# An offset of its own, modulo 256 bytes, for each ring slot of split weight chunks

## The chip, the cores and the metric

The kernel runs on one core of a Trainium2 chip. The metric is the device time of one execution in microseconds (us); of several runs the median is given.

## What is computed

One decoder layer on 256 tokens of width 1024, all in float32. A SwiGLU feed-forward of width 2816, then a mixing layer with two branches side by side (a Mamba-2 state-space branch and a differential attention branch) that a sigmoid gate merges, then a second SwiGLU feed-forward. Around each stands an RMS norm before and one after. Cut to what matters:

```python
h = h + 0.5 * rmsnorm(swiglu(rmsnorm(h, ffn1_pre_g), w_gate, w_up, w_down), ffn1_post_g)
u = rmsnorm(h, mix_pre_g)
z, xbc, dt_raw, q, k, v, gate_logits = split(u @ w_in)
...
merged = gates[0] * y_ssd + gates[1] * y_att
h = h + rmsnorm(merged @ w_out, mix_post_g)
h = h + 0.5 * rmsnorm(swiglu(...), ffn2_post_g)
```

Almost all of the work is the product of the 256 tokens with some 32 million weights, each of which is read once from HBM.

## The kernel before, in words

**Precision by splitting.** A float32 product is made of three matmuls in the faster fp32r format. Each weight chunk and each activation is split into a high part, the value rounded to fp32r, and a low part, what the rounding left. Of the four products the three larger are added up: hi times hi, lo times hi and hi times lo.

**Weight chunks.** The weights come in chunks of 128 partitions by 2048 floats (8 KB per partition, 1 MB in all). For each chunk:
- `load` (L226) issues a DMA on SyncE's queue into a raw tile (L237).
- `hi` (L260) copies the raw tile to a tile `whi` on ScalarE, with rounding (L263).
- `lo` (L267) subtracts `whi` from the raw tile on VectorE and writes `wlo` (L270).
- `take` (L372) gives the pair to the matmuls, and has the next chunks prepared some way ahead.

There are 134 such pairs in the program; some (named `whiq` and `wloq`) come from sums of raw chunks, since part of the feed-forward uses a seven-product form (L309).

**The matmuls.** `mm_t` (L383, its matmuls on L390, L391 and L393) uses the chunk as the stationary operand and streams 256 token columns; 28 chunks in the mixing layer go that way. `mm_nat` (L395, its matmul on L404) and `mm_n` (L605, its matmul on L619) use the activations as the stationary operand and stream 512 columns of the chunk; the other 106 go that way.

**Where split chunks stand.** `ring` (L198) gives out the tiles. For each of the two kinds, `whi` and `wlo`, there are three slots of 8 KB per partition in the pool `sb`, which lives for the whole program, taken in turn. In the feed-forwards a fourth slot of each kind lies in the stage's own pool, and each fourth chunk of the kind goes there: 9 in each feed-forward. So of the 134 pairs 112 stand in the six slots of `sb`, 18 in the stages' slots, and 4, at the seams between stages, in half tiles of the stage (`blocks`, L245).

**Addresses.** Before the first `whi` slot and behind the last `wlo` slot `gap` (L195) puts a tile of 32 floats, 128 bytes, and has GpSimd set it to zero (L196). By the program's memory map the first gap begins at byte 84512 of each partition, which is 32 modulo 256. The starts of the tiles that matter here, modulo 256 (inside them matmuls, copies and subtractions begin at multiples of 256, but for the shifted reads of a convolution):

| tiles | start modulo 256 |
|---|---|
| three `whi` slots and three `wlo` slots in `sb` | 160 |
| raw tiles, the activations `u`, all tiles of the stage pools (the fourth slots, `gh`, `gl`, `v`, `sqy` and so on) | 160 |
| `k2` tiles (`sg`, `us`, `aT`, `wdt` and so on) | 224 |
| `h` and `ident` | 128 |
| `ones` | 192 |

**Order.** `own_order` (L427) has TensorE, ScalarE, VectorE and SyncE run in the order of the program text in the feed-forwards; GpSimd's queue is put in order by the framework's scheduler. In the mixing layer the scheduler orders more of the engines, up to L1383, where TensorE is taken into the text's order again. At the start GpSimd computes the inverse norms of the two token blocks (`rstd_of`, L502: L505 and L506), scales the second block (`unit`, L548: L551 `un_f`) and makes a diagonal (`diag`, L554); the gaps' zeros stand among these in its queue.

Of the kernel before, what the change touches and what calls it, by code (L numbers as in the profile page):

```python
# [14 lines left out]
F32 = mybir.dt.float32  # L15
F32R = mybir.dt.float32r
# [8 lines left out]
P = 128  # L25
T = 256
D = 1024
# [20 lines left out]
BG_US = 3.15  # L48
GATE_US = 1.35
SSD_US = 1.55  # L50
GROUPS = "hnsns"
BREAK, STOP = object(), object()

# [2 lines left out]
def tile_hybrid_layer(ctx: ExitStack, tc: tile.TileContext, x, ffn1_pre_g, ffn1_w_gate, ffn1_w_up,  # L56
# [4 lines left out]
    nc = tc.nc  # L61
    const = ctx.enter_context(tc.tile_pool(name="const", bufs=1))
    sb = ctx.enter_context(tc.tile_pool(name="sb", bufs=1))
# [69 lines left out]
    def ffn_chunks(wg, wu, wd):  # L133
# [3 lines left out]
        c0 = 512  # L137
        for kind in GROUPS:
            if kind == "h":
# [46 lines left out]
    raws, pairs, taken, rings = [], {}, [0], {}  # L186
# [5 lines left out]
    def mixing(c):  # L192
        return mix_first <= c < mix_last

    def gap(name):  # L195
        nc.gpsimd.memset(sb.tile([P, 32], F32, tag=name, name=name, bufs=1), 0.0)  # L196

    def ring(kind, n, more, name, c, dt=F32):  # L198

        first = kind not in rings  # L200
        i = rings.get(kind, 0) % (n + more)
        rings[kind] = rings.get(kind, 0) + 1
        if i < n or stage[1][1] != FFN_K4 or mixing(c):
            if first and kind == "whi":
                gap("gap0")
            t = sb.tile([P, 2 * D], dt, tag=kind, name=name, bufs=n)
            if first and kind == "wlo":
                gap("gap1")
            return t
        return stage[1][0].tile([P, 2 * D], dt, tag=kind, name=name, bufs=more)  # L210

    class Raw:
# [32 lines left out]
    def blocks(name, c, nj, nc_):  # L245

        if c in seams:
            n = nj // 2
            ts = [k4([P, n, nc_], f"{name}{q}", F32R) for q in range(2)]
            return lambda j, m: ts[j // n][:, j % n:j % n + m, :]  # L250
        t = ring(name[:3], SPLIT_BUFS, SPLIT_MORE, name, c, F32R).rearrange("p (j c) -> p j c", j=nj)
        return lambda j, m: t[:, j:j + m, :]
# [190 lines left out]
    h = const.tile([P, 2, D], F32, name="h")  # L443
# [35 lines left out]
    for name, v in (("mx", mix_pre_g), ("f2", ffn2_pre_g),  # L479
                    ("ng", ssd_norm_g), ("cb", ssd_conv_b), ("sg", da_subln_g)):  # L480
        n = v.shape[1] // P
# [236 lines left out]
    def ffn(post_v, tag, norm, ready, turned, then, at, ws=None, **kw):  # L718
# [21 lines left out]
        def later(n, f):  # L740
            due.append((slot[0] + n, f))
# [85 lines left out]
        for n, f in ((0, lambda: turned_back(sgs[0], 0, gh, gl)), (2, lambda: turned_back(sgs[1], 1, gh, gl)),  # L827
                     (8, then)):
            later(n, f)
        if "s" in GROUPS:  # L830
            for n in range(6):
                later(2 * n, lambda: next(making, None))
        else:
            norm.pu1 = norm.us = None
        for n, kind in enumerate(GROUPS):
            m = 2 if kind == "h" else 4
# [185 lines left out]
    dt = const.tile(shp, F32, name="dt")  # L1022
# [362 lines left out]
    def natural(name, n, hi, lo, evict, us, then=lambda: None):  # L1385


        accs = [pj(f"{name}{b}") for b in range(2)]
        for i in range(n):
            w = take()  # L1390
            for b in range(2):
                bs = slice(b * P, (b + 1) * P)
                mm_nat(accs[b], w, (lambda k: hi(k)[:, bs], lambda k: lo(k)[:, bs]), i * 4, i == 0, i == n - 1, "u")
                if i == n - 1:
                    evict(b, accs[b])
                back.run(us)
            if i == 0:
                then()
# [22 lines left out]
    for q in range(2):  # L1421
# [3 lines left out]

        natural(f"pws{q}", 4, lambda j: yh[j // 4][:, j % 4, :], lambda j: yl[j // 4][:, j % 4, :], gated, SSD_US)
    yh = yl = None
# [4 lines left out]
    def turn_merged(n):  # L1432

        for q, b, t, mh, ml in merges[:n]:
            pt = bg([P, 4, P], f"pmg{q}{b}")
            for m in range(4):
                nc.tensor.transpose(pt[:, m, :], t[:, m * P:(m + 1) * P], ident)
            bs = slice(b * P, (b + 1) * P)
            split(mh[:, :, bs], ml[:, :, bs], pt)
        del merges[:n]  # L1440
# [5 lines left out]
    for q in range(2):  # L1446
# [4 lines left out]
        def merge(b, acc):  # L1451
# [5 lines left out]
        natural(f"pwd{q}", 2, lambda j: oh[j // 4][:, j % 4, :], lambda j: ol[j // 4][:, j % 4, :], merge,  # L1457
                SSD_US if q == 0 else 0.0, (attended, lambda: turn_merged(2))[q])

# [51 lines left out]
```

## Time and profile before

| | |
|---|---|
| median of 3 runs | 765.84 us (765.19 to 766.61) |
| the profiled execution | 764.21 us |
| its span, from the first to the last instruction | 762.5 us |
| TensorE matmuls | 4113, busy 739.7 us (97%) |
| VectorE busy | 563.4 us (74%) |
| ScalarE busy | 431.3 us (57%) |
| GpSimd busy | 41.8 us (5%) |
| HBM traffic | 137 MB, 180 GB/s over the span |

The profile names the engines PE (TensorE, with PEld for its weight loads), DVE (VectorE), ACT (ScalarE), POOL (GpSimd) and SP (SyncE). L404 is line 404 of the kernel. A group of instructions has its line, engine and operation, output and inputs (`out<-in`; for a matmul the moving operand stands ahead of the stationary one), shape and count; then busy time in us, the mean length of one in ns, and the idle time of the engine ahead of them with what ended it. Matmuls overlap in the pipeline, so the mean length of one is longer than the time from one start to the next. In a piece of the chain or of the timeline the first number is the start in us, the second the length in us.

### The profile page before, as it was taken

Reading aid. Unit: us, or ns where it says so; the run is one execution under the profiler, and the core shown is the slowest. Engines: PE = TensorE matmul, PEld = TensorE weight load, DVE = VectorE, ACT = ScalarE, POOL = GpSimd, SP = SyncE. Lnnn points to the kernel's source line nnn. Section 1 sums busy time; section 2 is a strip of 40 time slices with the busy share of each in tenths; the row PEclk is TensorE's granted clock in tenths of the full one; section 3 lists DMA queues with packets and bytes.
Section 4 is the critical chain, followed back from the end, with each engine's and each line's share of the span. In section 5 each row is a group of like instructions: output and inputs, shape, how many; then the busy total and the mean of one; then the engine's idle time right before and its main releaser. Section 6 shows DMA issues by size and latency. Waiting matters only on the chain.

```text
span 762.5 us, 10271 instructions
## 1 busy us (share of the span) xinstructions
PE 739.7 (97%) x4113; PEld 628.7 (82%) x4113; DVE 563.4 (74%) x666; ACT 431.3 (57%) x583; POOL 41.8 (5%) x74
## 2 busy tenths in 40 slices
PE   8999899999989999999999999999999999999996
PEld 6878687788769999989999777888887888888885
DVE  6788897853657787777877878685777999988332
ACT  7543746743545455676967545685365657566321
POOL 6000000000141000000000000000013000000000
PEclk9999999999999999999999999999999999999999
DMA  8950755864345856565456454544565817549301
GB/s 315 318 200 0 272 169 169 336 210 141 111 125 181 263 179 182 176 190 160 139 174 191 161 198 135 191 164 133 201 221 166 282 50 248 193 167 358 110 1 55
DMA packets 77889, 137.92 MB, mean 181 GB/s; under 512 B 2749, under 2 KB 35601, under 8 KB 77841
## 3 DMA queue, kind: packets, MB, share of 16 engines
q1 hardware_dynamic: 75168, 129.51, 50.6%
q0 software_dynamic: 2368, 7.22, 3.2%
q8 instruction: 32, 0.52, 0.3%
q10 hardware_dynamic: 304, 0.53, 0.2%
q14 instruction: 17, 0.13, 0.0%
HBM read 136.17 MB, written 1.08 MB: 180 GB/s over the span
## 4 chain that ended last, share of the span: by engine, by line
PE 81%; DVE 7%; ACT 6%; issue 3%; POOL 1%; DMA 1%; SPq 0%; DVEq 0%; ACTq 0%; POOLq 0%
PE acc_f L619 15%; PE pu_f L404 6%; PE pg_f L404 5%; PE pws L404 5%; PE pgt L404 4%; PE pa_f L404 4%; ACT whi L263 3%; PE pn_f L404 3%; PE pwd L404 3%; DVE wlo L270 3%; PE pd_f L404 2%; PE pz L391 2%; PE pz L390 2%; PE pz L393 2%; PE pxs L391 2%
## 5 line engine op out<-in xcount | busy, mean ns | idle before, releaser
L270 DVE TENSOR_TENSOR wlo<-raw,whi 128x2048 fp32r<-128x2048 f32 (+2 forms) x116 | 243.5, 2109 | 94.3 <-ACT whi L263 92.7
L263 ACT CAST whi<-raw 128x2048 fp32r<-128x2048 f32 (+2 forms) x116 | 202.5, 1763 | 130.1 <-PE acc_f L619 38.0
L263 ACT CAST whiq<-raw 128x2048 fp32r<-128x2048 f32 x24 | 45.9, 1914 | 27.4 <-PE pu_f L404 11.3
L270 DVE TENSOR_TENSOR wloq<-raw,whiq 128x2048 fp32r<-128x2048 f32 x24 | 54.7, 2286 | 5.8 <-ACT whiq L263 5.8
L619 PE MATMUL acc_f<-whi,gh_f 128*128 128x512 f32 x160 | 51.6, 392 | 0.0
L619 PE MATMUL acc_f<-wlo,gh_f 128*128 128x512 f32 x160 | 51.3, 391 | 0.2 <-DVE wlo L270 0.2
L619 PE MATMUL acc_f<-whi,gl_f 128*128 128x512 f32 x160 | 51.4, 390 | 0.0
L404 PE MATMUL pgt<-whi,u_mx 128*128 128x512 f32 x128 | 35.1, 401 | 0.4 <-DVE gt L1415 0.4
L619 PEld LDWEIGHTS acc_f<-wlo,gh_f 128*128 128x128 f32 x160 | 29.9, 188 | 6.7 <-DVE wlo L270 0.6
L619 PEld LDWEIGHTS acc_f<-whi,gl_f 128*128 128x128 f32 x160 | 30.0, 188 | 6.2
L619 PEld LDWEIGHTS acc_f<-whi,gh_f 128*128 128x128 f32 x160 | 29.8, 188 | 6.2 <-ACT whi L263 0.2
L404 PE MATMUL pg_f<-whi,u_f 128*128 128x512 f32 x128 | 32.5, 397 | 1.2 <-DVE sg_f L777 1.2
L390 PE MATMUL pz<-u_mx,whi 128*128 128x256 f32 x128 | 32.0, 286 | 0.0
L391 PE MATMUL pz<-u_mx,whi 128*128 128x256 f32 x128 | 31.9, 286 | 0.0
L390 PE MATMUL pxs<-u_mx,whi 128*128 128x256 f32 x128 | 31.8, 286 | 0.0
L404 PE MATMUL pu_f<-whi,u_f 128*128 128x512 f32 x128 | 31.8, 391 | 0.0
L391 PE MATMUL pxs<-u_mx,whi 128*128 128x256 f32 x128 | 31.4, 283 | 0.0
L404 PEld LDWEIGHTS pg_f<-whi,u_f 128*128 128x128 f32 x128 | 23.4, 188 | 6.4 <-DVE sg_f L777 1.6
L404 PEld LDWEIGHTS pgt<-whi,u_mx 128*128 128x128 f32 x128 | 23.3, 188 | 6.4 <-issue 1.3
L404 PEld LDWEIGHTS pu_f<-whi,u_f 128*128 128x128 f32 x128 | 24.0, 188 | 5.0
L391 PEld LDWEIGHTS pz<-u_mx,whi 128*128 128x128 f32 x128 | 24.5, 192 | 0.5 <-issue 0.5
L390 PEld LDWEIGHTS pz<-u_mx,whi 128*128 128x128 f32 x128 | 24.5, 191 | 0.5 <-issue 0.5
(372 smaller groups left out, 1646.8 us busy)
## 6 DMA issues: line engine op xcount, KB each, us to landing
raw<-in_w_in_dram SPq DMA_DIRECT2D x40, 1024.0 KB, 5.3
raw<-in_ffn_w_down_dram SPq DMA_DIRECT2D x22, 1024.0 KB, 5.3
raw<-in_ffn_w_gate_dram SPq DMA_DIRECT2D x18, 1024.0 KB, 5.8
raw<-in_ffn_w_up_dram SPq DMA_DIRECT2D x18, 1024.0 KB, 5.2
raw<-in_ssd_w_branch_dram SPq DMA_DIRECT2D x8, 1024.0 KB, 5.0
raw<-in_ffn_w_up_dram SPq DMA_DIRECT2D x8, 512.0 KB, 5.8
acb<-acd POOLq DMA_DIRECT2D x8, 512.0 KB, 4.7
raw<-in_da_w_branch_dram SPq DMA_DIRECT2D x4, 1024.0 KB, 5.0
```

The lines of the kernel that those rows point to most:

```text
L263: i = nc.scalar.copy(got["hi"](j, step), src()[:, j:j + step, :])
L270: nc.vector.tensor_sub(got["lo"](j, step), src()[:, j:j + step, :], got["hi"](j, step).bitcast(F32))
L390: nc.tensor.matmul(acc[m], wh(j)[:, cs], ah(k0 + j), start=first and j == ks[0], stop=False)
L391: nc.tensor.matmul(acc[m], wh(j)[:, cs], al(k0 + j), start=False, stop=False)
L393: nc.tensor.matmul(acc[m], wl(j)[:, cs], ah(k0 + j), start=False, stop=last and j == ks[-1])
L404: nc.tensor.matmul(acc, a(k0 + j), b(j), start=first and i == 0, stop=last and i == 11, skip_group_check=go_on)
L619: nc.tensor.matmul(acc[b][q], x_[:, ts], w_(kt)[:, halves[q]], start=i == 0 and kt == 0 and x_ is ah and w_ is wh, stop=i == n - 1 and kt ...
```

## The change

The two gaps of 128 bytes become seven smaller ones, one ahead of each of the six slots and one behind the last. `STEPS` has their sizes in bytes, `GAP_END` the last. Each slot gets a tag of its own, with one buffer, and the slots are taken in turn by a counter of each kind. When a split chunk is first asked for, all gaps and all six slots are made at once (`home` tiles), so that they lie one behind the other, and the home tiles are then let go, so that the chunks take their places. The `whi` slots begin at 64, 96 and 128 modulo 256, the `wlo` slots at 192, 224 and 0. The gaps add up to 256 bytes as before.

```diff
+STEPS = {"whi": (32, 32, 32), "wlo": (64, 32, 32)}
+GAP_END = 32
...
-    def gap(name):
-        nc.gpsimd.memset(sb.tile([P, 32], F32, tag=name, name=name, bufs=1), 0.0)
+    homes, slots = {}, {k: 0 for k in STEPS}
+
+    def gap(name, size):
+        if size:
+            nc.gpsimd.memset(sb.tile([P, size // 4], F32, tag=name, name=name, bufs=1), 0.0)
 
     def ring(kind, n, more, name, c, dt=F32):
 
-        first = kind not in rings
         i = rings.get(kind, 0) % (n + more)
         rings[kind] = rings.get(kind, 0) + 1
         if i < n or stage[1][1] != FFN_K4 or mixing(c):
-            if first and kind == "whi":
-                gap("gap0")
-            t = sb.tile([P, 2 * D], dt, tag=kind, name=name, bufs=n)
-            if first and kind == "wlo":
-                gap("gap1")
-            return t
+            if kind not in STEPS:
+                return sb.tile([P, 2 * D], dt, tag=kind, name=name, bufs=n)
+            if not homes:
+                for k in STEPS:
+                    for slot in range(n):
+                        gap(f"gap_{k}{slot}", STEPS[k][slot])
+                        homes[k, slot] = sb.tile([P, 2 * D], F32R, tag=f"{k}{slot}", name=f"home_{k}{slot}", bufs=1)
+                gap("gap_end", GAP_END)
+                homes.update((h, None) for h in list(homes))
+            slot = slots[kind] % n
+            slots[kind] += 1
+            return sb.tile([P, 2 * D], dt, tag=f"{kind}{slot}", name=name, bufs=1)
         return stage[1][0].tile([P, 2 * D], dt, tag=kind, name=name, bufs=more)
```

## The prediction

> **What bounds the kernel now.** I read the page first: the busy shares, the granted clock and the chain that ended last.
>
> ```profile
> span 762.5 us, 10271 instructions
> PE 739.7 (97%) x4113; PEld 628.7 (82%) x4113; DVE 563.4 (74%) x666; ACT 431.3 (57%) x583; POOL 41.8 (5%) x74
> PEclk9999999999999999999999999999999999999999
> PE 81%; DVE 7%; ACT 6%; issue 3%; POOL 1%; DMA 1%; SPq 0%; DVEq 0%; ACTq 0%; POOLq 0%
> ```
>
> TensorE is busy 97% of the span, at full clock, and carries 81% of the chain. ScalarE and VectorE carry 13% of it. The question is therefore how fast TensorE runs in its long stretches, and whether an address could make that better or worse. Two pieces of the chain in order of time (start, length, what) say the first, and a count of the instructions of two lines (span, busy, number, for PE and PEld) says how many matmuls go at that pace.
>
> ```profile
> 147.61 49.47 PE acc_f L619 x218
> 302.33 0.96 PE pxs L393 x8
> ```
>
> ```profile
> 0.00:762.50 762.50, 377.46 (x1584) 292.70 (x1584) 1.00 0.54 181
> ```
>
> ```profile
> 0.00:762.50 762.50, 144.84 (x624) 116.41 (x624) 1.00 0.54 181
> ```
>
> The 218 matmuls of 512 columns take 49.47 / 218 = 0.227 us each, the ones of 256 columns 0.96 / 8 = 0.120 us. The slope between the two is 0.107 us for 256 columns, 2.4 columns per ns, and 0.013 us is a constant per matmul. So in a long stretch nothing is lost to a slow read: whatever is lost comes at breaks. Lines 404 and 619 together issue 1584 + 624 = 2208 matmuls of 512 columns; these read a split chunk as the moving operand. In the 256-column ones (L390 to L393) the chunk is the stationary operand.
>
> **What is moved.** In the program's memory map raw tiles, the six ring slots, the transposed activations u and all stage tiles start at 160 modulo 256; the k2 tiles at 224, h and ident at 128, ones at 192. The change moves only the six slots. It replaces two gaps of 128 bytes by 32+32+32+64+32+32+32 = 256 bytes, so all that lies behind keeps its address. The raw tiles that the DMAs fill don't move. Slots were taken in turn before and are after, so no wait is added and none goes. What is left are two questions: does any instruction that touches a slot run at another rate, and where do five more memsets go.
>
> **VectorE and ScalarE on the slots.** Here are the costs now (count, then busy us and mean ns), and below them an operation whose three operands share one offset (L1150, all at 160) beside one that mixes 224 and 160 (L381 reads us_f at 224 and u_f at 160, writes u_f at 160).
>
> ```profile
> L270 DVE TENSOR_TENSOR wlo<-raw,whi 128x2048 fp32r<-128x2048 f32 x98 | 224.1, 2290 | 92.1 <-ACT whi L263 91.7
> L263 ACT CAST whi<-raw 128x2048 fp32r<-128x2048 f32 x98 | 186.1, 1909 | 125.3 <-PE acc_f L619 38.0 <-PE pxs L391 22.1 <-PE pwd L404 13.7
> L270 DVE TENSOR_TENSOR wlo<-raw,whi 128x1024 fp32r<-128x1024 f32 x14 | 16.5, 1216 | 2.2 <-PE acc_f L619 1.3 <-ACT whi L263 1.0
> L1150 DVE TENSOR_TENSOR sqy<-sqy 128x512 f32<-128x512 f32 x4 | 2.7, 686 | 0.0
> L381 DVE TENSOR_TENSOR u_f<-us_f,u_f 128x512 fp32r<-128x512 f32 x4 | 2.7, 685 | 0.1
> ```
>
> Mixed and equal offsets take 685 and 686 ns, 0.2% apart. From 1024 to 2048 elements the split's subtraction grows by 1074 ns, 1.05 ns per element, the same slope as from 512 to 1024 (1216 - 686 = 530 ns, 1.04): no stall now that could go. On the chain, by line on the page, the two splitting lines hold 3% each:
>
> ```profile
> PE acc_f L619 15%; PE pu_f L404 6%; PE pg_f L404 5%; PE pws L404 5%; PE pgt L404 4%; PE pa_f L404 4%; ACT whi L263 3%; PE pn_f L404 3%; PE pwd L404 3%; DVE wlo L270 3%; PE pd_f L404 2%; PE pz L391 2%; PE pz L390 2%; PE pz L393 2%; PE pxs L391 2%
> ```
>
> That is 6% of 762.5 = 46 us. At the 0.2% just seen this is 0.1 us in either direction; I take 0. To matter they would have to lose 1.5 us, 3.3% of their length, and no pair of rows shows that.
>
> **TensorE on the slots.** The nearest pair is of 128-column matmuls: warm has both operands in ident (128 and 128), po has v at 160 moving and aT at 224 stationary.
>
> ```profile
> L469 PE MATMUL warm<-ident x28: 275/276/582, 1.6 to 7.7; 128*128 128x128 f32 x28
> ```
>
> ```profile
> L1246 PE MATMUL po<-v,aT x16: 274/276/276, 449.9 to 519.6; 128*128 128x128 f32 x16
> ```
>
> Both medians are 276 ns. So a distance of 64 bytes costs and gains nothing. After the change the moving chunk stands 32, 64 or 96 bytes away from its stationary operand, on either side; only 64 has a row, and only in a short matmul. For the 512-column matmul I bound it by the spread of the rows now:
>
> ```profile
> L404 PE MATMUL pgt<-whi,u_mx 128*128 128x512 f32 x128 | 35.1, 401 | 0.4 <-DVE gt L1415 0.4
> L404 PE MATMUL pg_f<-whi,u_f 128*128 128x512 f32 x128 | 32.5, 397 | 1.2 <-DVE sg_f L777 1.2
> L404 PE MATMUL pws<-whi,yh 128*128 128x512 f32 x64 | 18.3, 409 | 0.0
> L404 PE MATMUL pgt<-wlo,u_mx 128*128 128x512 f32 x64 | 17.2, 391 | 0.0
> ```
>
> The three groups that hold the matmuls behind breaks have means of 397 to 409 ns, the one inside a stretch 391. All operands are at 160 in all four rows, so the offset does not make that difference by itself. Lower bound: all of it goes, 10 ns x 128 + 6 x 128 + 18 x 64 = 3.2 us. Upper bound: 10 ns more on every 512-column matmul that reads a slot. By the code 106 chunks are used as moving operands, 84 of them in the ring, so 2208 x 84 / 106 = 1750 matmuls and 17.5 us. I take 0, since the row nearest in kind (276 against 276) shows none.
>
> The page "SBUF — State Buffer" of the Trainium skill (Who interferes with whom) speaks against any effect: only the port pair that VectorE shares with GpSimd causes contention, and "PE and ACT never wait on anyone". By that rule both bounds are 0; the pairs of rows above agree, for a distance of 64 bytes, and the other distances no run here shows yet.
>
> **The memsets.** GpSimd's timeline at the start:
>
> ```profile
> 5.14 0.30 POOL L505 TENSOR_SCALAR r_f<-ss_f 128x1 f32<-128x1 f32 x1 [3.60 <-ACT sq_f L500]
> 5.50 0.18 POOL L196 MEMSET gap<- 128x32 f32 x2
> 5.65 0.95 POOL L506 TENSOR_TENSOR r_f<-r_f,nhalf 128x1 f32<-128x1 f32 x1
> 8.00 0.30 POOL L505 TENSOR_SCALAR r_f<-ss_f 128x1 f32<-128x1 f32 x1 [1.41 <-DVE sq_f L542]
> 9.05 4.15 POOL L551 TENSOR_SCALAR un_f<-h,r_f 128x512 f32<-128x512 f32 x2
> ```
>
> Two memsets push the next start by 5.65 - 5.50 = 0.15 us, 0.075 us each; five more cost 0.38 us. L506 then ends at 6.60 + 0.38 = 6.98, and GpSimd still waits until 8.00 for the second block's squares: hidden under 1.41 us of idle time. On ScalarE the first to read its result r_f comes at 17.43:
>
> ```profile
> 17.43 0.74 ACT L419 ACTIVATE sg_f1b<-pn_f,r_f 128x512 f32<-128x512 f32 x1
> ```
>
> If the scheduler put the memsets behind 8.00 instead, un_f, which the chain passes, would come up to 0.38 us later. I take 0.
>
> **The sum.** 0 (VectorE, ScalarE) + 0 (TensorE) + 0 (memsets). The profiled execution took 764.21 us: its span of 762.5 and 1.7 around it. The median of the three runs is 765.84, 1.6 above it, so the forecast against the median is 765.84 + 0 = 765.8 us. About 0.2%, 1.5 us, is what a measurement of this kernel can tell from no change: the three runs lie 1.4 us apart.
>
> **The rivals.**
>
> A. Slower: moving and stationary reads that are now in step at 160 fall out of step, and a slot whose distance is bad makes its matmuls take 401 instead of 391 ns throughout. Place: the 512-column stretches, acc_f above all. A hi slot is read by 8 of 12 matmuls of a chunk, in every third chunk: 1750 x 2/3 / 3 = 389, at 10 ns 3.9 us, so 769.7; a lo slot 1.9 us; all six 17.5, 783.3. It decides from 1.5 us, 0.9 ns on each of the 1750. For it: the distances 32 and 96 have no row. Against it: 276 against 276 at 64.
>
> B. Faster: the stretched matmuls behind a break are reads that collide because both start at 160, and distance ends that. All of it is worth 3.2 us: 762.6. Half of it is needed to pass the bound. For it: 401 against 391 ns. Against it: within a stretch of 218 the same equal offsets run at 0.227 us, so equality alone is not the cause, and the first matmul behind a break is long anyway.
>
> C. The memsets land on the start's chain: 0.38 us, 766.2; still no change that can be told.
>
> D. The slots don't get the offsets named, because a home tile is not reused by the ring tile of its tag. Then the reads are as now or at some other offset: 765.8, or A or B in part.
>
> **How the numbers follow.** No change that can be told, with C and D inside it: 0.60. The rows at a distance of 64 are equal for VectorE and TensorE, but two of three distances lack a row, so A gets 0.20 and B, whose gain is capped at 3.2 us, also 0.20. The range reaches to B in full, 762.6, and to one bad hi slot of A, 769.7; what is left out is A with two bad slots or more, under 0.1, and a gain that no row prices. The likeliest case alone would be 764.3 to 767.4.
>
> **What would show it.** Right: the 98 subtractions stay at 2290 ns and the 98 casts at 1909; acc_f stays at 0.227 us per matmul in its long piece; pgt's hi row stays near 401 ns; seven memsets stand before 8.00 and un_f still starts at 9.05. A shows as 512-column rows at 395 to 401 ns inside stretches, B as hi rows near 391. The prediction is wrong if the span moves by over 1.5 us, above all if it moves with none of these rows: then the order or a wait has changed, which I hold to be impossible from the code.

## The result, and the profile after

| | before | after |
|---|---|---|
| median | 766.05 us (4 runs, 765.19 to 766.61) | 770.61 us (4 runs, 769.77 to 770.97) |
| ratio to before, 95% interval | | 1.0059 (1.0042 to 1.0076) |
| the profiled execution | 764.21 us | 770.75 us |
| its span | 762.5 us | 769.1 us |

The kernel became slower by 4.6 us, 0.6%, three times what the prediction named as the smallest difference that can be told, and above its range of 762.6 to 769.7. The two profiled executions lie 6.5 us apart, their spans 6.6, some 2 us more than the medians: the profiled run of before is faster than all four of its timed ones. So the medians say how much, and the traces say where. Of 17 further runs of before (taken beside the first experiments), the four with a mean granted clock of 0.998 took 764.0 to 764.6 us, the thirteen with 0.995 or 0.996 took 764.6 to 767.7.

The page of the changed kernel, its head and the engines' shares of the chain:

```profile
span 769.1 us, 10276 instructions
...
PE 747.4 (97%) x4113; PEld 627.4 (82%) x4113; DVE 563.9 (73%) x666; ACT 431.1 (56%) x583; POOL 41.5 (5%) x79
...
PE 82%; DVE 6%; ACT 6%; issue 3%; POOL 1%; DMA 1%; SPq 0%; DVEq 0%; ACTq 0%; POOLq 0%
```

TensorE has as many matmuls as before and is busy 747.4 - 739.7 = 7.7 us longer. VectorE's and ScalarE's busy times are within 0.5 us of those of before. So the time came on inside TensorE's own work, and not as a wait for another engine. The long piece of the chain, and the windows of the two lines with 512-column matmuls (L404 is now L414, L619 is L629; the columns are as before):

```profile
148.72 50.41 PE acc_f L629 x218
```

```profile
0.00:800.00 800.00, 384.89 (x1584) 293.90 (x1584) 1.00 0.52 172
```

```profile
0.00:800.00 800.00, 147.53 (x624) 116.38 (x624) 1.00 0.52 172
```

The same 218 matmuls take 50.41 instead of 49.47 us: 0.231 each, not 0.227. The lines' busy times grow by 7.4 and 2.7 us; the number is the same, and the clock rounds to 1.00 in both.

The rounding hides one difference. In the trace of after the granted clock was 0.50 for 3.4 us, where the mixing layer's first matmuls stand; in the trace of before it was not. Here are that window of after (its length; busy time and count of PE, PEld, DVE, ACT and POOL; the granted clock, the DMA share, GB/s), and TensorE's timeline from the first `pn_mx` on, after and then before:

```profile
214.70:218.10 3.40, 3.40 (x11) 2.75 (x9) 2.17 (x8) 3.40 (x9) 1.46 (x3) 0.50 1.27 296
```

```profile
214.69 2.03 PE L414 MATMUL pn_mx<-whi,u_mx 128*128 128x512 f32 x4
216.51 1.85 PE L414 MATMUL pn_mx<-wlo,u_mx 128*128 128x512 f32 x4
```

```profile
212.63 1.17 PE L404 MATMUL pn_mx<-whi,u_mx 128*128 128x512 f32 x4
213.64 1.08 PE L404 MATMUL pn_mx<-wlo,u_mx 128*128 128x512 f32 x4
```

The first four start (216.51 - 214.69) / 4 = 0.455 us apart in place of 0.2525. Matmul by matmul (the two kernels issue them in the same order) this stretch costs 1.6 us that the offsets have no part in. So 5.0 of the 6.6 us between the spans are left for the change, which is close to the medians' 4.6.

Where it happens can be seen inside one stretch. TensorE's timeline (start, length of the group, what), at the place where `acc_f` goes over from a chunk in a fourth slot, which the change left at 160, to one in ring slots (its hi half at 64, its lo half at 192), which it does at 162.85 (five groups of two are left out in each half):

```profile
160.13 0.61 PE L629 MATMUL acc_f<-whi,gh_f 128*128 128x512 f32 x2
...
162.85 0.63 PE L629 MATMUL acc_f<-whi,gh_f 128*128 128x512 f32 x2
...
165.64 0.63 PE L629 MATMUL acc_f<-whi,gh_f 128*128 128x512 f32 x2
```

From 160.13 to 162.85 twelve matmuls start 2.72 / 12 = 0.2267 us apart; from 162.85 to 165.64 twelve more, 2.79 / 12 = 0.2325 apart. Nothing waits there, and the matmuls are of the same kind: only the chunk's slot differs.

Below, a matmul's **interval** is the time from its start to the next one's. Added up over the trace, the intervals of all 512-column matmuls went from 526.5 to 535.5 us (+9.0), and those of the 256-column ones (with 128 columns of weights) from 168.8 to 166.3 (-2.5). Together that is +6.5, and the span grew by 6.6. The stretch at half clock lies in 512-column matmuls; without it they grew by 7.4, both together by 4.9, and the span by 5.0. So two effects of opposite sign make the result, and the second was in none of the cases of the prediction.

One group by form of before that the prediction did not show, and then those of the changed kernel, for the steps on VectorE, ScalarE and both kinds of matmuls:

```profile
L619 PE MATMUL acc_f<-whi,gh_f 128*128 128x512 f32 x160 | 51.6, 392 | 0.0
```

```profile
L280 DVE TENSOR_TENSOR wlo<-raw,whi 128x2048 fp32r<-128x2048 f32 x98 | 224.1, 2290 | 93.5 <-ACT whi L273 93.1
L273 ACT CAST whi<-raw 128x2048 fp32r<-128x2048 f32 x98 | 185.8, 1906 | 127.2 <-PE acc_f L629 39.4 <-PE pxs L401 21.3 <-PE pwd L414 14.3
...
L629 PE MATMUL acc_f<-whi,gh_f 128*128 128x512 f32 x160 | 52.1, 395 | 0.0
...
L414 PE MATMUL pgt<-whi,u_mx 128*128 128x512 f32 x128 | 35.6, 405 | 0.2 <-DVE gt L1425 0.2
...
L414 PE MATMUL pgt<-wlo,u_mx 128*128 128x512 f32 x64 | 17.4, 394 | 0.0
...
L403 PE MATMUL pxs<-u_mx,wlo 128*128 128x256 f32 x128 | 17.6, 279 | 0.0
```

The subtraction takes the same 2290 ns, the cast 1906 instead of 1909: slots at six different offsets cost those two engines nothing. `acc_f` went from 392 to 395 ns, `pgt` from 401 to 405 and from 391 to 394. The mean length is a poor measure here, since matmuls overlap; it shows 3 or 4 ns of what is 5 to 7 in the intervals. GpSimd's timeline at the start:

```profile
5.44 0.18 POOL L201 MEMSET gap_whi<- 128x8 f32 x3
5.55 0.19 POOL L201 MEMSET gap_wlo<- 128x16 f32 x3
5.67 0.10 POOL L201 MEMSET gap_end<- 128x8 f32 x1
5.74 0.57 POOL L516 TENSOR_TENSOR r_f<-r_f,nhalf 128x1 f32<-128x1 f32 x1
7.99 0.31 POOL L515 TENSOR_SCALAR r_f<-ss_f 128x1 f32<-128x1 f32 x1 [1.69 <-DVE sq_f L552]
...
9.05 4.15 POOL L561 TENSOR_SCALAR un_f<-h,r_f 128x512 f32<-128x512 f32 x2
```

The seven memsets are over ahead of 5.8, and `un_f` starts at 9.05 as before. The instruction behind them starts at 5.74, 0.09 us later than before; the prediction had 0.38.

### The profile page after: what moved, and what is told of

It is laid out like the page before. It is cut to its first block, busy times and chain, and to the rows that moved or that the text cites. A ratio compares the mean times of both kernels' runs of the same rounds, so it can differ in the third digit from the quotient of the medians.

```text
span 769.1 us, 10276 instructions
## 1 busy us (share of the span) xinstructions
PE 747.4 (97%) x4113; PEld 627.4 (82%) x4113; DVE 563.9 (73%) x666; ACT 431.1 (56%) x583; POOL 41.5 (5%) x79
## 4 chain that ended last, share of the span: by engine, by line
PE 82%; DVE 6%; ACT 6%; issue 3%; POOL 1%; DMA 1%; SPq 0%; DVEq 0%; ACTq 0%; POOLq 0%
PE acc_f L629 15%; PE pu_f L414 6%; PE pg_f L414 5%; PE pws L414 5%; PE pgt L414 4%; PE pa_f L414 4%; PE pn_f L414 4%; ACT whi L273 3%; PE pwd L414 3%; PE pd_f L414 2%; DVE wlo L280 2%; PE acc_mx L629 2%; PE pxs L400 2%; PE pxs L401 2%; PE pxs L403 2%
## 5 line engine op out<-in xcount | busy, mean ns | idle before, releaser
L629 PE MATMUL acc_f<-whi,gh_f 128*128 128x512 f32 x160 | 52.1, 395 | 0.0
L629 PE MATMUL acc_f<-whi,gl_f 128*128 128x512 f32 x160 | 52.1, 395 | 0.0
L629 PE MATMUL acc_f<-wlo,gh_f 128*128 128x512 f32 x160 | 51.9, 394 | 0.2 <-DVE wlo L280 0.2
L629 PEld LDWEIGHTS acc_f<-wlo,gh_f 128*128 128x128 f32 x160 | 29.9, 188 | 7.5 <-DVE wlo L280 0.6
L414 PE MATMUL pgt<-whi,u_mx 128*128 128x512 f32 x128 | 35.6, 405 | 0.2 <-DVE gt L1425 0.2
L629 PEld LDWEIGHTS acc_f<-whi,gl_f 128*128 128x128 f32 x160 | 30.0, 188 | 6.8
L629 PEld LDWEIGHTS acc_f<-whi,gh_f 128*128 128x128 f32 x160 | 29.7, 188 | 6.8
L414 PE MATMUL pg_f<-whi,u_f 128*128 128x512 f32 x128 | 33.0, 399 | 0.9 <-DVE sg_f L787 0.9
L414 PE MATMUL pu_f<-whi,u_f 128*128 128x512 f32 x128 | 32.3, 395 | 0.0
L414 PEld LDWEIGHTS pgt<-whi,u_mx 128*128 128x128 f32 x128 | 23.3, 188 | 6.7 <-issue 1.3
L414 PEld LDWEIGHTS pg_f<-whi,u_f 128*128 128x128 f32 x128 | 23.5, 188 | 6.4 <-DVE sg_f L787 1.3
L414 PEld LDWEIGHTS pu_f<-whi,u_f 128*128 128x128 f32 x128 | 24.0, 188 | 5.5
L414 PE MATMUL pn_f<-whi,u_f 128*128 128x512 f32 x96 | 25.1, 395 | 0.0
L414 PE MATMUL pa_f<-whiq,S_f 128*128 128x512 f32 x96 | 24.6, 398 | 0.0
```

What stands on the lines that cost most here:

```text
L414: nc.tensor.matmul(acc, a(k0 + j), b(j), start=first and i == 0, stop=last and i == 11, skip_group_check=go_on)
L629: nc.tensor.matmul(acc[b][q], x_[:, ts], w_(kt)[:, halves[q]], start=i == 0 and kt == 0 and x_ is ah and w_ is wh, stop=i == n - 1 and kt ...
```

## The experiments

**Theory 1**: the distance modulo 256 between the addresses of a matmul's moving operand and its weights sets TensorE's pace, pictured as its own two reads getting in each other's way. The experiments test the distance; the picture they can't see. Its rivals: the absolute start of a tile decides, whatever the other operand's; or another engine's or a DMA's traffic is needed, which meets TensorE's reads at the new offsets. "In step" below means a distance that is a multiple of 256. The intervals are worked out from the starts in the traces.

### m1: trains of matmuls alone

The layer is replaced by trains of 40 matmuls from two tiles, with no other work beside them. `om` shifts the moving operand, `os` the stationary one:

```python
for i in range(40):
    m, s = om + i % 4 * 512, os + i % 8 * 256
    nc.tensor.matmul(acc[:, :cols], sta[:, s:s + P], mov[:, m:m + cols], start=i == 0, stop=i == N - 1)
```

The first letter is the number of columns (n 512, m 256, k 384, l 128), the second the shift of the moving operand in bytes (a 0, b 32, c 64, d 96, e 128, f 160, g 192, h 224, i 16, j 256, k 512); p, q and r shift both operands, by 32, 96 and 160; s and t shift the stationary one, by 64 and 192.

> This kernel leaves the layer out: it copies x to the output and runs trains of 40 matmuls on TensorE alone, no other engine at work. Moving and stationary tile both start at 128 modulo 256; in train na (512 columns) and ma (256 columns) they are in step, in b to h the moving operand is read 32, 64, 96, 128, 160, 192 or 224 bytes further on, in i 16, j 256, k 512 bytes; in p, q, r both are moved by 32, 96, 160 bytes, in s and t the stationary one by 64 and 192. k and l are trains of 384 and 128 columns. Theory 1 (the distance modulo 256 between the address of the moving operand and that of the stationary tile loaded beside it sets TensorE's pace, with nothing else needed): na, nj, nk, np, nq, nr 0.227 us per matmul; nb to nh 0.230 to 0.235; ma 0.120 and mb to mh 0.115 to 0.120. Theory 2 (ScalarE's and VectorE's traffic on the slots slows TensorE): all n trains 0.227, all m trains 0.120. Theory 3 (the absolute start counts, not the distance): np, nq, nr differ from na, and ns, nt are as na.

TensorE's timeline, a row for each train:

```profile
26.55 9.23 PE L49 MATMUL na<-mov,sta 128*128 128x512 f32 x40
35.61 9.50 PE L49 MATMUL nb<-mov,sta 128*128 128x512 f32 x40
44.95 9.33 PE L49 MATMUL nc<-mov,sta 128*128 128x512 f32 x40
54.11 9.49 PE L49 MATMUL nd<-mov,sta 128*128 128x512 f32 x40
63.44 9.49 PE L49 MATMUL ne<-mov,sta 128*128 128x512 f32 x40
...
128.23 4.96 PE L49 MATMUL ma<-mov,sta 128*128 128x256 f32 x40
133.02 4.88 PE L49 MATMUL mb<-mov,sta 128*128 128x256 f32 x40
...
156.69 4.70 PE L49 MATMUL mg<-mov,sta 128*128 128x256 f32 x40
161.23 4.89 PE L49 MATMUL mh<-mov,sta 128*128 128x256 f32 x40
...
256.75 4.58 PE L49 MATMUL la<-mov,sta 128*128 128x128 f32 x40
261.16 4.63 PE L49 MATMUL lb<-mov,sta 128*128 128x128 f32 x40
265.63 4.63 PE L49 MATMUL lc<-mov,sta 128*128 128x128 f32 x40
```

Take the difference of two rows' starts by 40: in step (35.61 - 26.55) / 40 = 0.2265 us, at 32 bytes (44.95 - 35.61) / 40 = 0.2335, at 64 bytes 0.2290, at 96 0.2333. With 256 columns it is the other way round: 0.1198 in step, 0.1135 at 192 (mg). With 128 columns `lb` gives 0.1118. The settled intervals in ns (at 256 and 512 bytes they are those of 0):

| distance | 0 | 16 | 32 | 64 | 96 | 128 | 160 | 192 | 224 |
|---|---|---|---|---|---|---|---|---|---|
| 512 columns | 226.7 | 231.7 | 233.3 | 228.9 | 233.3 | 233.2 | 234.4 | 233.3 | 233.3 |
| 256 columns | 120.0 | 113.3 | 117.8 | 117.8 | 120.1 | 118.7 | 117.4 | 113.3 | 118.3 |
| 128 columns | 111.7 | 111.7 | 111.7 | 111.7 | 111.7 | 111.7 | 111.7 | 111.7 | 111.7 |

With both operands shifted alike (p, q, r) the intervals are those of distance 0; with only the stationary one shifted by 64, a distance of 192, they are 233.3 and 113.3. So, as far as these starts go, the distance decides and not the absolute start, and TensorE needs no other engine for it: from 26 to 376 us no other engine is busy and the DMA share is 0.00. Both rivals fall as explanations of the loss. Theory 1's own bounds were a little too narrow: 228.9 ns at 64 lies under its 0.230 us, 113.3 under its 0.115, 120.1 at 96 at its upper edge. The trains also show that a 128-column pair can't tell anything of distances: the mean lengths of those rows are 274 or 275 ns at all eleven shifts.

### e1: the change's code, with all slots back at 160

```diff
-STEPS = {"whi": (32, 32, 32), "wlo": (64, 32, 32)}
-GAP_END = 32
+STEPS = {"whi": (128, 0, 0), "wlo": (0, 0, 0)}
+GAP_END = 128
```

> The code of the change with gaps of 128, 0, 0, 0, 0, 0 and 128 bytes: all six slots at 160 modulo 256, as before the change, with a tag and a counter for each slot and home tiles. Theories 1, 2 and 3: the time of the kernel before, 766.0 us within 0.2%, acc_f at 0.227 us per matmul. Rival (the tags, the home tiles or the memsets cost the time): 770.6 us.

765.45 us, ratio 0.9997 (0.9986 to 1.0009) to the 765.32 of before beside it. The long piece in the chain of waits:

```profile
147.85 49.44 PE acc_f L629 x218
```

0.227 us per matmul again. So the tags, the home tiles and the order of the ring cost nothing; the whole result hangs on the offsets.

### e3_32: all six slots at 32

```diff
+STEPS = {"whi": (0, 0, 0), "wlo": (0, 0, 0)}
+GAP_END = 256
```

> All six slots at one common offset, 32 modulo 256, 128 bytes from every stationary tile; raw, u and stage tiles stay at 160. Theory 1: out of step everywhere, by the neighbours in the trace after (distance 96: 234.2 ns, 160: 233.3 ns, against 227.0) 1750 matmuls of 512 columns lose some 7 ns, 12 us, and 1344 of 256 columns gain 2 to 3 ns, 3 us: 774 to 776 us. Theory 2 in the form that slots must differ from the raw tiles: also slower, by some 5 us, 771. Rival (it is the differing of the slots among themselves that costs): 766 us.

770.87 us, ratio 1.0071 (1.0058 to 1.0085): +5.5 us against 765.32, the sign that theory 1 expected and little over half of the size. By the time alone the rival of the raw tiles (771) did better; m1 and e4_stage speak against it, not this run. The distance of ring slots to activations is 128 here, and the settled interval of their matmuls is 232.7 ns, as in the train (233.2). The price of one is right, then, and the count was wrong. What it left out: in before only 1697 of 2207 intervals are below 229 ns; 413 are at 229 to 300 and 97 longer, all of them at breaks or behind one. Those have nothing more to lose. 1750 x 1697 / 2207 = 1346 matmuls by 5.7 ns are 7.7 us, and the intervals of all 512-column ones grew by 7.8 (7.3 without a stretch at half clock, which this trace has too); the 256-column ones gave back 0.8. This account was made behind the result.

### e4_stage: slots at 160, the other operand moved

```diff
+STEPS = {"whi": (128, 0, 0), "wlo": (0, 0, 0)}
+GAP_END = 192
```

Now all that lies behind the slots moves by 64 bytes: the stages' tiles, `gh` and `gl` among them, begin at 224, while the slots and `u` stay at 160.

> The six slots stay at 160 modulo 256 as before the change; the last gap is 192 instead of 128 bytes, so that all tiles of the stage pools (gh, gl, yh, oh, mh, the fourth slots, two raw tiles) go to 224; u and three raw tiles stay at 160. Theory 1: matmuls with a stationary tile of the stage and a moving one in a slot are 192 bytes apart, 232 instead of 227 ns; some 1050 of them, 850 with a slot: 4.5 us, and the fourth slots with u 64 bytes apart, 230 ns: in all 770 to 771 us; acc_f at 0.231 to 0.232, pu_f with u mostly at 0.227. Theory 2: the slots lie to the raw tiles and to each other as before: 766 us, acc_f at 0.227.

770.95 us, ratio 1.0075 (1.0063 to 1.0088), as theory 1 expected. The long piece of the chain, and two groups by form:

```profile
148.26 50.58 PE acc_f L629 x218
```

```profile
L629 PE MATMUL acc_f<-whi,gh_f 128*128 128x512 f32 x160 | 52.3, 395 | 0.0
...
L414 PE MATMUL pu_f<-wlo,u_f 128*128 128x512 f32 x64 | 17.2, 390 | 0.0
```

The slots stand where they stood before, and `acc_f`, whose weights now come from 224, takes 0.232 us per matmul all the same; `pu_f`, whose activations and most of whose chunks are at 160, has 390 ns, as before. No ring slot needs to move for the loss. That is theory 1 in the layer itself.

### e2_lo and e2_hi: one half of the change each

```diff
+STEPS = {"whi": (128, 0, 0), "wlo": (32, 32, 32)}
+GAP_END = 32
```

> The change for the lo slots alone: hi slots at 160 modulo 256 as before, lo slots at 192, 224 and 0. Theory 1, by the trains: 583 matmuls of 512 columns at distances 32, 64 and 96 lose 6.6, 2.2 and 6.6 ns, 3.0 us; 448 of 256 columns at 224, 192 and 160 gain 1.7, 6.7 and 2.6 ns, 1.6 us: 1.4 us slower than before at the most, 765.5 to 767 us. Theory 2 (slots out of step with the raw tiles): a third to a half of the change's 4.6 us, 767 to 768 us.

```diff
+STEPS = {"whi": (32, 32, 32), "wlo": (32, 0, 0)}
+GAP_END = 128
```

> The change for the hi slots alone: hi slots at 64, 96 and 128 modulo 256, lo slots at 160. Theory 1, by the trains: 1167 matmuls of 512 columns at distances 160, 192 and 224 lose 7.7, 6.6 and 6.6 ns, 8.1 us; 896 of 256 columns at 96, 64 and 32 gain 0, 2.2 and 2.2 ns, 1.3 us: up to 6.8 us, and as common offset 32 gave about half of what was worked out this way, 769 to 772 us. Theory 2: half of the change's time or a little more, 768 to 769 us.

The lo slots alone took 770.0 us, 1.0053 (1.0037 to 1.0068); the hi slots alone 769.29, 1.0050 (1.0035 to 1.0066), against 765.93 for before beside them. The second came as expected by theory 1. The first lies above what either theory had: a third of the matmuls cost almost all that the change costs, +4.1 of +4.6 us, and the halves add up to 7.4. The price is not one per out-of-step matmul. The long piece with the lo slots alone:

```profile
148.89 50.27 PE acc_f L629 x218
```

All 218 matmuls average 0.2306 us, though two of three are in step. In the intervals of that trace, the matmuls in step that follow an out-of-step one take 232.6, 231.5, 230.6, 229.8, 230.3, 230.4, 229.1, 228.3, 228.0 and 226.8 ns: an in-step matmul is not fast at once. So theory 1 got an addition, 1a: TensorE needs some eight or nine matmuls in step to settle at 226.7.

### m3: a few matmuls out of step

Trains of 144, in which the last so many of each dozen are shifted by 32 bytes: a none, b 1 of 12, c 4 of 12, d 8 of 12, e all, f 4 of 48.

```python
m = i % 4 * 512 + (off // 4 if period - i % period <= out_ else 0)
```

> Trains of 144 matmuls on TensorE alone, the layer left out, x copied to the output; n trains 512 columns, m trains 256, out-of-step ones read 32 bytes further on. In a none of 12 are out of step, in b the last of each 12, in c the last 4, in d the last 8, in e all 12, in f the last 4 of each 48. The lo slots alone had cost nearly as much as all six. Theory 1a (a matmul in step takes some eight matmuls to settle behind one out of step, as in the trace of the lo slots, where the first behind it take 232.6, 231.5, 230.6 ns and the ninth 226.8): na 0.2267, ne 0.2333 us, and nc well above a third of the way, 0.231 to 0.233 instead of 0.2289, nb 0.230 instead of 0.2272, nf 0.2275 to 0.229. Theory 1b (each matmul by its own distance alone): na 0.2267, nb 0.2272, nc 0.2289, nd 0.2311, ne 0.2333, nf 0.2272 us; the lo slots' cost then comes from something else than TensorE.

```profile
50.39 32.80 PE L48 MATMUL na<-mov,sta 128*128 128x512 f32 x144
83.03 33.40 PE L48 MATMUL nb<-mov,sta 128*128 128x512 f32 x144
116.27 33.60 PE L48 MATMUL nc<-mov,sta 128*128 128x512 f32 x144
149.71 33.64 PE L48 MATMUL nd<-mov,sta 128*128 128x512 f32 x144
183.19 33.76 PE L48 MATMUL ne<-mov,sta 128*128 128x512 f32 x144
216.79 33.00 PE L48 MATMUL nf<-mov,sta 128*128 128x512 f32 x144
249.63 17.45 PE L48 MATMUL ma<-mov,sta 128*128 128x256 f32 x144
```

By differences of starts over 144: none 0.2267, 1 of 12 0.2308, 4 of 12 0.2322, 8 of 12 0.2325, all 0.2333, 4 of 48 0.2281. One matmul in twelve brings 4.1 of the 6.6 ns that all twelve bring. Behind it, the intervals of those in step run 233, 233, 236, 224, 231, 236, 228, 232, 231, 227, 227 ns. That is the run of numbers that stands behind a break in the kernel before, from 496.16 us on: 335, then 235, 233, 236, 224, 231, 236, 228, 232, 231, 227, 232, with all operands at 160. TensorE's timeline there, four matmuls to a row:

```profile
496.16 1.20 PE L404 MATMUL pws<-whi,yh 128*128 128x512 f32 x4
497.19 1.08 PE L404 MATMUL pws<-wlo,yh 128*128 128x512 f32 x4
498.11 1.08 PE L404 MATMUL pws<-whi,yl 128*128 128x512 f32 x4
```

The first four take 0.2575 us each with the break's long one, the next four 0.230, before the stretch is at its pace. So a break and a matmul out of step cost the same few ns on the matmuls behind them: 1a holds.

### m2: finer distances, and trains that alternate

Distances of 4 to 240 bytes as in m1, and trains in which every other matmul has its stationary operand 64 or 96 bytes on (`s = i % 8 * 256 + (off // 4 if i % 2 else 0)`): if the collision were with a matmul's own weights, the shifted ones would be long, and if with the next one's, those in step.

> Trains of 40 matmuls on TensorE alone again, the layer left out, x copied to the output. n trains have 512 columns, m trains 256; distance a 4, b 8, c 16, d 48, e 80, f 112, g 144, h 176, i 208, j 240 bytes, k 0. Then four trains in which the stationary tile stands in turn in step with the moving one (its matmul writes nxsame, nysame, mxsame, mysame) and 64 (x) or 96 (y) bytes further on (nxapart and so on). Theory 1: k at 0.2267 and 0.120 us as in the first trains; every other n train between 0.2267 and 0.235, every other m train between 0.113 and 0.120; only k in step. If it is the next matmul's weight load, read beside the moving stream, that counts, then the matmul in step with its own weights but beside a load 96 bytes apart (nysame) is the long one, 392 to 398 ns against 389; if its own weights count, nyapart is. Theory 3, that only certain absolute starts are slow, was already out by the first trains.

With 512 columns no distance is as fast as 0 (226.7): 4 bytes 236.8, 8 bytes 233.3, 16 bytes 231.6, 80 and 112 bytes 231.1, 48, 144, 176 and 240 bytes 233.3 to 233.4, 208 bytes 234.6. With 256 columns 112 bytes gave 113.3, 4 and 8 bytes 123.3 and 126.7. So 4 bytes lies outside theory 1's bounds for 512 columns, and 4 and 8 bytes do for 256. The alternating trains did not decide their question: both kinds are long (233.5 and 231.5 ns for 64 bytes, 230.8 and 229.2 for 96), as 1a would have it, and with whose weights the distance counts stays open.

### e7_u: the distances chosen by kind of matmul

By m1, 192 is, with 16, the best for the 256-column matmuls (113.3 for 120.0), and 64 is the least bad for 512 columns. In the mixing layer `u` is the moving operand against stationary chunks in 256-column matmuls; elsewhere it is stationary. So slots, stages and the feed-forwards' `u` all stand at 160, and `u` of the mixing layer at 96: 96 - 160 is 192 modulo 256, and a chunk at 160 that streams over weights at 96 has a distance of 64.

```diff
+STEPS = {"whi": (128, 0, 0), "wlo": (0, 0, 0)}
...
+    u_taken = [0]
+
+    def u_tile(name, apart):
+        slot = u_taken[0] % 2
+        u_taken[0] += 1
+        o = ((0, 48), (16, 0))[slot][apart]
+        t = sb.tile([P, 2 * D + (48, 16)[slot]], F32R, tag=f"u8{'ab'[slot]}", name=name, bufs=1)
+        return t[:, o:o + 2 * D].rearrange("p (j h t) -> p j h t", j=4, h=2)
...
-            uT[i] = sb.tile([P, 4, 2, T], F32R, tag="u8", name=f"u{i}_{tag}", bufs=2)
+            uT[i] = u_tile(f"u{i}_{tag}", tag == "mx")
...
-                o8 = sb.tile([P, 4, 2, T], F32R, tag="u8", name="o8", bufs=2)
+                o8 = u_tile("o8", False)
```

The last gap stays at 32 bytes. The padding is paid for by that and by giving one kind of six-element tiles 5 buffers in place of 10.

> A version made from theory 1. All slots and stage tiles at 160 modulo 256 as before the change, so that the 512-column matmuls stay in step; only the activations u of the mixing layer, the moving operand of the 256-column matmuls, stand at 96, so that these are 192 bytes apart (113.3 ns in the trains, 115.0 in the profile after, against 120.0). 1344 of them gain 5.0 to 6.7 ns, 6.7 to 9.0 us; 288 matmuls of 512 columns that have this u as stationary tile, 64 bytes apart, lose 2.2 to 2.8 ns, 0.8 us at the most. Theory 1: 757 to 760 us, faster than before the change. Theory 2: 765.5 us.

759.45 us, ratio 0.9920 (0.9902 to 0.9937): 6.5 us faster than the 765.93 of before beside it, 11.2 faster than the change, and as expected. One row of the groups by form, before and in e7_u:

```profile
L391 PE MATMUL pxs<-u_mx,whi 128*128 128x256 f32 x128 | 31.4, 283 | 0.0
```

```profile
L401 PE MATMUL pxs<-u_mx,whi 128*128 128x256 f32 x128 | 30.2, 277 | 0.0
```

The row has 277 ns in place of 283. Its settled interval is 113.9 ns, and the 512-column matmuls are at 227.0, but 229.2 where they stream over `u` of the mixing layer. The totals of all kernels, in us, from the intervals ("both" and "span" against before; the last column is what a stretch of 3.4 us at half clock near 215 us, which four of the traces have, costs in the span, and of this in the 512-column matmuls):

| kernel | 512 columns | 256 columns | both | span | half clock |
|---|---|---|---|---|---|
| before | 526.5 | 168.8 | | | 0 |
| e1 | 526.4 | 168.8 | -0.1 | 0.0 | 0 |
| after | 535.5 | 166.3 | +6.5 | +6.6 | 1.6, 1.6 |
| e2_lo | 534.0 | 167.7 | +6.4 | +6.6 | 1.6, 1.6 |
| e2_hi | 532.6 | 166.7 | +4.0 | +3.7 | 0 |
| e3_32 | 534.3 | 168.0 | +7.0 | +7.3 | 1.2, 0.5 |
| e4_stage | 532.4 | 168.8 | +5.9 | +6.8 | 1.4, 0.6 |
| e7_u | 526.6 | 163.0 | -5.7 | -6.6 | 0 |

The matmul intervals account for the span within 1 us in every kernel, with the stretch and without it. These are single traces; e2_lo has no more than 4.1 us by its medians.

## Why the prediction was wrong

**The step that failed** is "TensorE on the slots": "So a distance of 64 bytes costs and gains nothing", and "I take 0, since the row nearest in kind (276 against 276) shows none". That row is not near in kind. In m1 a 128-column matmul takes 111.7 ns at every distance, and its mean length stays at 274 or 275, so that pair would have read 276 against 276 whatever the offsets do. With 512 columns the distances of the change cost 2.2 ns (64 bytes) to 7.7 (160 bytes) per settled matmul of the trains. Added up, the term that was taken as 0 was +7.4 us for the 512-column matmuls at full clock and -2.5 for the others.

**A second reading failed with it**: "0.013 us is a constant per matmul. So in a long stretch nothing is lost to a slow read". At a distance of 192 two matmuls of 256 columns take 2 x 113.3 = 226.6 ns, as long as one of 512 at its best. So the 0.120 us of before held a loss of 6.7 ns per matmul, 9.0 us over the 1344, and e7_u won 5.8 us of it back. Two rows with both operands in step could not tell a constant from a loss.

**A row that seems to tell, and does not.** `pdt` streams 256 columns of `u`, at 160, over weights in `wdt_h`, a `k2` tile at 224: a distance of 192. In the view of that tile, before and after (count, then shortest, median and longest length in ns):

```profile
L1009 PE MATMUL pdt<-u_mx,wdt_h x8: 276/277/281, 229.1 to 232.9; 128*32 128x256 f32 x8
```

```profile
L1019 PE MATMUL pdt<-u_mx,wdt_h x8: 280/282/283, 232.8 to 236.7; 128*32 128x256 f32 x8
```

The 277 ns of before, where the 256-column rows with both operands at 160 have means of 283 to 289, look like the effect. But the change moves neither of its operands, and after it the row has 282: its last eight intervals average 113.4 ns before and 120.0 after. Its weights have only 32 columns, and for this kind the distance alone doesn't set the pace. So this row of before could not have told either.

**Rival A** had the mechanism as far as it is known, moving and stationary operands that fall out of step, and its place, the 512-column stretches. Its price was 10 ns per matmul for every slot that is bad. All six slots are bad: 233.0 to 234.2 ns at distances of 96 and 160 and 224, 232.3 at 32, 232.4 at 192 and 229.8 at 64, against 227.0. By A's sum for six slots, 17.5 us, the change would have been at 783.3. Four things make it 7.4: 3 to 7 ns instead of 10; a quarter of the matmuls stand at a break or behind one and are slow anyway; these came out 1.2 us shorter in all; and against this, 1a charges the fourth-slot chunks, which did not move, 228.5 ns. The gain of 2.5 us on the 256-column matmuls then goes off. A price in proportion to a slot's matmuls was wrong in kind as well: by e2_lo and m3 a few matmuls out of step cost most of what all cost. For the three lo slots A's price gives 1750 / 3 x 10 ns = 5.8 us, and their trace has +5.9 on the 512-column matmuls at full clock; since all six give 7.4 and not 17.5, that agreement is luck.

**Rival B** is refuted. The 413 stretched intervals of before are settling behind breaks; m3's in-step matmuls behind a single one out of step show the same run of numbers, and no distance of the trains runs 512 columns below 226.7 ns. After the change 1693 intervals are at 229 to 300 ns.

**The Trainium skill's rule.** By "SBUF — State Buffer" of the Trainium skill (Who interferes with whom) TensorE has two independent read ports, for the moving operand and for weights, and waits on nobody. That no other engine is in play this case bears out: m1 shows the loss with none at work. That the two operands' addresses therefore can't matter, which is how the prediction used the rule, it does not: their distance alone moves a 512-column matmul from 226.7 to as much as 236.8 ns. The measurement decides.

**What was right**: VectorE and ScalarE at 0 (2290 and 1906 ns); the memsets at 0, hidden in GpSimd's wait for 7.99, so C did not occur; no order or wait that the tags and home tiles could have changed costs anything (e1). D did not occur either: the pace changes from slot to slot as the offsets do. The sign that the prediction set for A, 512-column rows at 395 to 401 ns inside stretches, came at its lower edge: `acc_f` at 395, `pgt`'s lo row at 394.

**What stays open**: whether it is a collision of reads at all, and if so of what, with a matmul's own weights or the next one's; why 256 columns gain from the distances at which 512 lose; why 256 columns at 16 bytes settled at 113.3 ns in m1 and at 116.6 in m2, and `pdt` at 113.4 and 120.0 at the same addresses. For 256 columns, then, the distance is not all that counts.

## What to carry to other kernels

Where TensorE is the bound and streams long operands, look at the start addresses of moving and stationary tiles: in this case equal starts modulo 256 were best for 512 columns, a distance of 192 (or 112) for 256 columns, and choosing both by kind was worth 0.8%. Before a pair of rows serves as evidence that something has no effect, ask whether that pair could show it at all. Before two traces are set against each other, look at the granted clock in short windows: here a stretch of 3.4 us, which the mean hardly shows (0.997 against 0.998), was 1.6 of 6.6 us. And when matmuls overlap, take their pace from differences of starts divided by counts, not from mean lengths; where no row bears on the question, a train of 40 matmuls for each case answers it in 10 us.

## What the runs showed of the hardware

- The interval of an fp32r matmul with 128 columns of weights depends on the distance of its operands' addresses modulo 256: 226.7 to 236.8 ns for 512 columns, 113.3 to 126.7 for 256 (m1, m2), 111.7 always for 128 (m1).
- After a break, or after a single matmul out of step, the next eight to ten matmuls of 512 columns run at 224 to 236 ns (m3) before 226.7 is reached; one such in twelve costs 4.1 ns on the mean of all.
- For 256 columns equal starts are among the slowest cases: 120.0 ns, against 113.3 at a distance of 192 or 112.
- VectorE and ScalarE did not feel the offsets: 2290 ns before and after for the subtraction, 1909 and 1906 for the cast.
- At a granted clock of 0.50 the first four `pn_mx` matmuls started 0.455 us apart, against 0.2525 at full clock (after, before).
